# Other places for the low weight blocks of a split float32 matmul, and another order of its three products

## The chip, the cores and the metric

The kernel runs on one core of one Trainium2 chip. The metric is the device time of one execution in microseconds. Before the change it is 2366.06 us, the median of 3 runs that lie between 2365.84 and 2366.32 us.

## The reference

A trunk of two layers works on 256 tokens and 16 learned meta tokens of width 2048. Every layer projects with one combined matrix, runs two groups of attention heads side by side (bidirectional gated linear attention in chunks, and neighbourhood attention on a 64-wide grid), projects back, and follows with a squared-ReLU MLP. Cut to what matters:

```python
def _layer(h, w_in, gla_w_up, gla_b_up, gla_norm_w, na_rel_bias, w_out,
           ln1_w, ln1_b, w_ff1, w_ff2, ln2_w, ln2_b):
    proj = jnp.einsum('bld,dp->blp', h, w_in)
    ...
    gq, gk, gv, gr, glr, nq, nk, nv = jnp.split(proj, points, axis=-1)
    y_gla = _gla_mixer(gq, gk, gv, gr, glr, gla_w_up, gla_b_up, gla_norm_w)
    y_na = _na_mixer(nq, nk, nv, na_rel_bias).astype(h.dtype)
    mix = jnp.einsum('blm,md->bld', jnp.concatenate([y_gla, y_na], axis=-1), w_out)
    h = _layer_norm(DEEPNORM_ALPHA * h + mix, ln1_w, ln1_b)
    ff = jnp.einsum('blf,fd->bld', jnp.square(jax.nn.relu(jnp.einsum('bld,df->blf', h, w_ff1))), w_ff2)
    return _layer_norm(DEEPNORM_ALPHA * h + ff, ln2_w, ln2_b)
```

The four large weights are 2048 x 6176, 2048 x 2048, 2048 x 8192 and 8192 x 2048 per layer, all float32. The meta tokens are dropped from the output, so the second layer needs its result for the 256 tokens alone.

## The kernel before

**Splitting.** Every large product runs on TensorE in the type float32r, with both operands split into a high part (the value cast to float32r) and a low part (the value less its high part). Three products are summed in PSUM: high weights by high activations, high weights by low activations, low weights by high activations.

**Weight tiles.** The weights come from HBM in tiles of 128 partitions x 1024 float32 (`WB`), eight blocks of 128 columns. `order` (line 149) yields them in the order of use and `weights` (line 168) keeps the tile in use and the one after it made. `made` (line 174) starts the DMA into `raw` from SyncE's queue, has ACT cast `raw` into `wh` (line 180) and DVE subtract `wh` from `raw` into `wl` (line 181). Each of `raw`, `wh` and `wl` has three buffers in the pool `wst`, so a buffer is written again when the third tile before it has been used. `head` (line 186) does the same for the very first tile, together with two chunks of the input.

**Where things lie.** In `wh` and in `wl` block j stands at element 128 j, and each tile begins at a multiple of 256 bytes; so every block does. An activation chunk (`x`, `y` or `u`, 128 partitions) is a `Pair` of a high and a low part in one tile. In layer one, and for some products of layer two, the low part begins 288 elements (`PITCH`, 1152 bytes) after the high part. For most of layer two the pair is dense: 256 high columns, then 256 low ones, which one matmul can read as 512.

**Products.** Three functions issue them, all for one weight tile at a time.
- `eight` (line 205) has eight chunks by one output block, and is called by `by_m` (line 253). Where all 272 columns (tokens and meta tokens) are wanted, each chunk has two high products of 272 columns, on line 216: the weights' high block by the chunk's high part, then the same block by its low part. After these 16 come 8 low products on line 219, the low blocks by the high parts. Where 256 columns suffice (`once`, layer two), each chunk has one high product of 512 columns, on line 213, and after these 8 come 8 low products of 256 columns, on line 219, into the right half of the PSUM bank; `whole` or the eviction adds both halves.
- `by_k` (line 232) has two chunks by four (or eight) output blocks, for the first products after a normalisation, on line 246. Its order is its own.

A few calls use 274 or 258 columns, where two more carry a gain and a bias.

**Around them.** `by_m` evicts each finished block with ACT and DVE and calls `pump`, which hands out steps of two queues of generators (`fg`, `bg`): gates, attention, normalisation. Those steps are issued after the last subtraction into `wl` (`issue_after(self.wl)`), so a tile's split stands ahead of them in the queues.

Of the kernel before, what the change touches and what calls it, by code (L numbers as in the profile page):

```python
# [19 lines left out]
L = T + NM  # L20
DEPTH = 2
# [5 lines left out]
WB = 1024  # L27
# [10 lines left out]
MEET = 2  # L38
PAD = 40
PITCH = 288  # L40


class Pair(tuple):
# [10 lines left out]
class Trunk:  # L54
# [95 lines left out]
    def order(self):  # L150

        i, first = self.i, [(), (WB // 2, WB)]
        for l in range(DEPTH):
            groups = [i["win"][l, g] for g in range(12)] + [i["wout"][l, g] for g in range(4)]
            for half in range(2):
                groups += [i["wff1"][l, 8 * half + g] for g in range(8)] + [i["wff2"][l, half, g] for g in range(4)]
            if l == 0:
                for t in range(groups[0].shape[0]):
                    for w in groups[:2]:
                        yield w[t], first.pop(0) if first else (WB,)  # L160
                groups = groups[2:]
            for w in groups:
                for t in range(w.shape[0]):
                    yield w[t], (WB,)

    def weights(self):

        while len(self.ready) < 2:
            self.ready.append(self.made(*next(self.stream, (None, ()))))
        return self.ready.popleft()  # L170

    def made(self, ap, ends):
        if ap is None:
            return None
        nc = self.nc
        raw, wh, wl = (self.wp.tile([P, WB], d, name=nm, tag=nm)
                       for nm, d in (("raw", F32), ("wh", F32R), ("wl", F32R)))
        for c in map(slice, (0,) + ends, ends):
            nc.sync.dma_start(raw[:, c], ap[:, c])
            nc.scalar.copy(wh[:, c], raw[:, c])  # L180
            self.wl = nc.vector.tensor_tensor(wl[:, c], raw[:, c], wh[:, c].bitcast(F32), ALU.subtract).ins  # L181
        if not ends:
            self.head(ap, raw, wh, wl)
        return wh, wl

    def head(self, ap, raw, wh, wl):

        nc, q = self.nc, WB // 4
        both = self.xr.tile([P, 2, q + L], F32, name="head", tag="head", bufs=1)
        self.x[:2] = [self.pair(self.xp, "x", c) for c in range(2)]  # L190
        for c in range(2):
            nc.sync.dma_start(both[:, c], self.i["head"][:, c])
        nc.sync.dma_start(raw[:, 2 * q:], ap[:, 2 * q:])
        for c in range(2):
            at = slice(c * q, c * q + q)
            h, lo = (t[:, :L] for t in self.x[c])
            todo = [(both[:, c, q:], h, lo), (both[:, c, :q], wh[:, at], wl[:, at])]
            for args in todo[::-1] if c else todo:
                self.split(*args)
        for at in (slice(2 * q, 3 * q), slice(3 * q, WB)):  # L200
            nc.scalar.copy(wh[:, at], raw[:, at])
            self.wl = nc.vector.tensor_tensor(wl[:, at], raw[:, at], wh[:, at].bitcast(F32), ALU.subtract).ins

    def eight(self, ps, wh, wl, x, n, first, last, once):

        mm = self.nc.tensor.matmul
        c = lambda w, j: w[:, j * P:j * P + P]  # L210
        for j, v in enumerate(x):
            if once:
                mm(ps, lhsT=c(wh, j), rhs=v.once, start=first and not j, stop=False)  # L213
                continue
            for i in range(2):
                mm(ps[:, :n], lhsT=c(wh, j), rhs=v[i][:, :n], start=first and not i + j, stop=False)  # L216
        o = ps[:, T:] if once else ps[:, :n]
        for j, (h, _) in enumerate(x):
            mm(o, lhsT=c(wl, j), rhs=h[:, :T if once else n], start=False, stop=last and j == 7)  # L219

    def whole(self, parts):

# [7 lines left out]
    def by_k(self, acts, n, before, wide=False):  # L230

        ps = [self.pm.tile([P, 512], F32, name="mm", tag="mm") for _ in range(4)]
        if wide:
            ps += [self.bank() for _ in range(4)]
        nk = len(acts)
        for k in range(0, nk, 2):
            before(k)
            for g in range(0, len(ps), 4):
                wh, wl = self.weights()
                parts = ((wh, 0), (wh, 1), (wl, 0))  # L240
                order = [(j, p, m) for j in range(2) for p in range(3) for m in range(4)]
                by_output = k == nk - 2 or k == 0 and not wide
                order.sort(key=lambda o: (o[0], o[2] // 2) if wide and not k + g else (by_output and o[2], o[1] // 2))
                for j, p, m in order:
                    c = j * 512 + m * P
                    self.nc.tensor.matmul(ps[g + m][:, :n], lhsT=parts[p][0][:, c:c + P], rhs=acts[k + j][parts[p][1]][:, :n],  # L246
                                          start=k + j + p == 0, stop=k == nk - 2 and j + p == 3)
        return [p[:, :n] for p in ps]

# [930 lines left out]
```

## Time and profile before

| | |
|---|---|
| median of 3 runs | 2366.06 us |
| the profiled execution, whole | 2366.29 us |
| its span | 2364.5 us |
| instructions | 44607 |
| matmuls, and as many weight loads | 18180 |
| TensorE busy | 2356.2 us |
| VectorE (DVE) busy | 1520.8 us |
| ScalarE (ACT) busy | 1219.3 us |
| HBM read, mean over the span | 414.03 MB, 176 GB/s |

A row of a group gives the line of the kernel, the engine, the operation, output and inputs by the program's names, the shapes, the count; then busy time in us and the mean duration of one in ns; then the engine's idle time just before them and what ended it. PE is TensorE's matmuls, PEld its weight loads, which run beside matmuls. Matmuls are pipelined: one starts long before the one ahead of it has ended, so their durations do not add up, and a group's busy time is the union. In the order of time a row gives the start in us, the time from the first start to the last end, and the instructions merged into it; the distance between the starts of two rows that follow each other on an engine tells what the first one cost. Rows of one source line give the least, the median and the greatest duration.

### The profile page before, as it was taken

What the parts mean: (1) busy time and instruction counts of PE and PEld (TensorE: products, weight loads), DVE (VectorE), ACT (ScalarE), POOL (GpSimd) and SP (SyncE); (2) the same over time, 40 slices, a digit from 0 to 9 for tenths busy, and PEclk for the clock granted to TensorE, in tenths of its full rate; (3) what the DMA queues carried; (4) which work ended last, traced back from release to release, by engine and by line L of the source; (5) the groups of instructions that cost most, each with busy time, mean ns of one, the idle gap of its engine ahead of it and who ended that gap; (6) DMA issues with size and microseconds to landing.
All of it is one profiled execution on the core that took longest, in us unless ns stands there. A gap on an engine that the chain in (4) does not pass through costs nothing.

```text
span 2364.5 us, 44607 instructions
## 1 busy us (share of the span) xinstructions
PE 2356.2 (100%) x18180; PEld 2241.9 (95%) x18180; DVE 1520.8 (64%) x2432; ACT 1219.3 (52%) x2100; POOL 136.2 (6%) x200
## 2 busy tenths in 40 slices
PE   9999999999999999999999999999999999999998
PEld 9999999999999999999999899999988888888888
DVE  5588777775544455546576787778766455666654
ACT  5666664564433344444456666655644333444443
POOL 0021100100000000000030111101100000000000
PEclk9999999999999999999999999999999999999999
DMA  7454445555555555555555555455566666556664
GB/s 261 153 160 153 156 135 176 173 176 178 177 178 176 176 177 179 177 177 174 177 184 171 164 160 165 155 160 188 187 192 190 189 187 188 188 190 212 195 188 144
DMA packets 118301, 419.02 MB, mean 177 GB/s; under 512 B 13512, under 2 KB 14024, under 8 KB 118096
## 3 DMA queue, kind: packets, MB, share of 16 engines
q1 hardware_dynamic: 117808, 415.65, 55.8%
q8 instruction: 142, 2.33, 0.4%
q14 instruction: 63, 0.52, 0.1%
q10 hardware_dynamic: 288, 0.52, 0.1%
HBM read 414.03 MB, written 2.10 MB: 176 GB/s over the span
## 4 chain that ended last, share of the span: by engine, by line
PE 98%; DVE 1%; issue 0%; ACT 0%; POOL 0%; DVEq 0%; ACTq 0%; POOLq 0%
PE mm L216 35%; PE mm L219 29%; PE mm L213 22%; PE mm L246 6%; PE bg L246 1%; PE bg L757 1%; PE mm L696 1%; PE bg L557 0%; PE bg L403 0%; DVE wl L181 0%; PE mm L722 0%; PE mm L446 0%; PE bg L883 0%; PE bg L608 0%; PE bg L638 0%
## 5 line engine op out<-in xcount | busy, mean ns | idle before, releaser
L181 DVE TENSOR_TENSOR wl<-raw,wh 128x1024 fp32r<-128x1024 f32 (+1 forms) x768 | 941.8, 1227 | 621.5 <-ACT wh L180 618.4
L180 ACT CAST wh<-raw 128x1024 fp32r<-128x1024 f32 (+1 forms) x768 | 803.5, 1047 | 919.4 <-PE mm L216 367.7
L216 PE MATMUL mm<-x,wh 128*128 128x272 f32 (+2 forms) x4224 | 569.8, 287 | 0.0
L216 PEld LDWEIGHTS mm<-x,wh 128*128 128x128 f32 x4224 | 541.1, 188 | 0.8 <-PE mm L696 0.2
L219 PE MATMUL mm<-x,wl 128*128 128x272 f32 (+3 forms) x3264 | 466.9, 285 | 0.0
L219 PEld LDWEIGHTS mm<-x,wl 128*128 128x128 f32 x3264 | 437.5, 189 | 11.6
L213 PE MATMUL mm<-x,wh 128*128 128x512 f32 x1152 | 290.1, 394 | 0.0
L213 PEld LDWEIGHTS mm<-x,wh 128*128 128x128 f32 x1152 | 207.2, 189 | 37.9 <-PE mm L696 0.4
L219 PE MATMUL mm<-y,wl 128*128 128x272 f32 (+1 forms) x1408 | 200.5, 285 | 0.0
L219 PEld LDWEIGHTS mm<-y,wl 128*128 128x128 f32 x1408 | 189.5, 189 | 6.5
L216 PE MATMUL mm<-y,wh 128*128 128x272 f32 (+1 forms) x1440 | 193.3, 286 | 0.0
L216 PEld LDWEIGHTS mm<-y,wh 128*128 128x128 f32 x1440 | 184.3, 188 | 0.0
L213 PE MATMUL mm<-y,wh 128*128 128x512 f32 x688 | 172.6, 392 | 0.0
L219 PE MATMUL mm<-u,wl 128*128 128x272 f32 (+1 forms) x1024 | 145.8, 285 | 0.0
L213 PEld LDWEIGHTS mm<-y,wh 128*128 128x128 f32 x688 | 123.6, 189 | 21.9
L219 PEld LDWEIGHTS mm<-u,wl 128*128 128x128 f32 x1024 | 137.8, 189 | 4.8
L216 PE MATMUL mm<-u,wh 128*128 128x272 f32 (+1 forms) x1056 | 141.2, 286 | 0.0
L216 PEld LDWEIGHTS mm<-u,wh 128*128 128x128 f32 x1056 | 134.9, 188 | 0.0
L213 PE MATMUL mm<-u,wh 128*128 128x512 f32 x496 | 124.2, 392 | 0.0
L213 PEld LDWEIGHTS mm<-u,wh 128*128 128x128 f32 x496 | 89.2, 189 | 15.9
L246 PE MATMUL mm<-x,wh 128*128 128x272 f32 (+1 forms) x512 | 73.3, 288 | 0.0
L246 PEld LDWEIGHTS mm<-x,wh 128*128 128x128 f32 x512 | 67.9, 191 | 0.0
(273 smaller groups left out, 1856.5 us busy)
## 6 DMA issues: line engine op xcount, KB each, us to landing
raw<-in_wff SPq DMA_DIRECT2D x512, 512.0 KB, 3.6
raw<-in_win SPq DMA_DIRECT2D x190, 512.0 KB, 3.8
raw<-in_wout SPq DMA_DIRECT2D x64, 512.0 KB, 3.6
nb<-in_nab SPq DMA_DIRECT2D x16, 352.0 KB, 4.7
xraw<-in_xT SPq DMA_DIRECT2D x7, 272.0 KB, 5.2
out<-out SPq DMA_DIRECT2D x5, 256.0 KB, 3.2
brow<-in_norm SPq DMA_DIRECT2D x4, 256.0 KB, 4.8
gw<-in_wup SPq DMA_DIRECT2D x4, 196.0 KB
```

The lines of the kernel that those rows point to most:

```text
L180: nc.scalar.copy(wh[:, c], raw[:, c])
L181: self.wl = nc.vector.tensor_tensor(wl[:, c], raw[:, c], wh[:, c].bitcast(F32), ALU.subtract).ins
L213: mm(ps, lhsT=c(wh, j), rhs=v.once, start=first and not j, stop=False)
L216: mm(ps[:, :n], lhsT=c(wh, j), rhs=v[i][:, :n], start=first and not i + j, stop=False)
L219: mm(o, lhsT=c(wl, j), rhs=h[:, :T if once else n], start=False, stop=last and j == 7)
L246: self.nc.tensor.matmul(ps[g + m][:, :n], lhsT=parts[p][0][:, c:c + P], rhs=acts[k + j][parts[p][1]][:, :n], start=k + j + p == 0, stop=k ...
L696: nc.tensor.matmul(ps[hh][:, t * NKEY:t * NKEY + NKEY], lhsT=q[hs, NM + t * P:NM + t * P + P], rhs=k[hs, t, :], start=True, stop=True)
L757: nc.tensor.matmul(po[t][hs, :P], lhsT=v2[ts, hs] if rest else v1[:, t, hs], rhs=p2[ts, hh, :] if rest else p1[:, 2 * hh + t, :], start=re ...
```

## The change

`wl` becomes 1280 elements wide (`WIDE`), and the low blocks no longer stand side by side. A tile that only serves products of 512 and 256 columns (`once`) has its low blocks 16 elements from the start, with steps of 160 in a pair and 320 from pair to pair: at 64 and 192 bytes by turns, counted within 256 bytes. All other tiles have them at 0, 176, 320, 496 and so on: at 0 and 192 bytes by turns. The high blocks stay side by side.

So that `made` knows which layout to use, `order` yields with every tile whether it is `once`. The cast and the subtraction are written for pairs of blocks (`halves`, `pairs`), and the products take a block's address from `block`.

The order in `eight` comes from a string. For `once` it is as before, eight high products (`h`) and eight low ones (`w`). For the others it was 16 high products and then 8 low ones; now two chunks have their four high products (`h` with the chunk's high part, `l` with its low part) and then their two low ones (`w`), four times over. The order in `by_k` is as before; its low blocks have new places too.

The three wider buffers take 3 KB more of each partition. `dynamic_dma_scratch_size` goes from 8192 to 2048, which moves all tiles by a multiple of 256 bytes.

```diff
+WIDE = 1280
+LOWS = {True: (16, P + 32, 2 * P + 64), False: (0, P + 48, 2 * P + 64)}
+TURNS = {True: "hhhhhhhhwwwwwwww", False: "hlhlwwhlhlwwhlhlwwhlhlww"}
...
-    def made(self, ap, ends):
+    def made(self, ap, ends, once):
...
-        raw, wh, wl = (self.wp.tile([P, WB], d, name=nm, tag=nm)
-                       for nm, d in (("raw", F32), ("wh", F32R), ("wl", F32R)))
+        raw = self.wp.tile([P, WB], F32, name="raw", tag="raw")
+        wh, wl = self.wp.tile([P, WB], F32R, name="wh", tag="wh"), self.wp.tile([P, WIDE], F32R, name="wl", tag="wl")
+        wh, wl = self.blocks(wh, 0, P, 2 * P), self.blocks(wl, *LOWS[once])
         for c in map(slice, (0,) + ends, ends):
             nc.sync.dma_start(raw[:, c], ap[:, c])
-            nc.scalar.copy(wh[:, c], raw[:, c])
-            self.wl = nc.vector.tensor_tensor(wl[:, c], raw[:, c], wh[:, c].bitcast(F32), ALU.subtract).ins
+            self.halves(raw[:, c], wh, wl, slice(c.start // P, c.stop // P))
...
+    def blocks(self, flat, first, step, pair):
+
+        ap = lambda at, n: bass.AP(flat.tensor, flat.offset + first + at, [flat.ap[0]] + n + [[1, P]])
+        return ap, step, pair
+
+    def block(self, w, j):
+        ap, step, pair = w
+        return ap(j // 2 * pair + j % 2 * step, [])
+
+    def pairs(self, w, at):
+
+        ap, step, pair = w
+        return ap(at.start // 2 * pair, [[pair, (at.stop - at.start) // 2], [step, 2]])
+
+    def halves(self, src, wh, wl, at):
+        h, lo = (self.pairs(w, at) for w in (wh, wl))
+        r = src.rearrange("p (g b c) -> p g b c", b=2, c=P)
+        self.nc.scalar.copy(h, r)
+        self.wl = self.nc.vector.tensor_tensor(lo, r, h.bitcast(F32), ALU.subtract).ins
...
     def eight(self, ps, wh, wl, x, n, first, last, once):
...
-        c = lambda w, j: w[:, j * P:j * P + P]
-        for j, v in enumerate(x):
+        seen = dict.fromkeys("hlw", 0)
+        for i, kind in enumerate(TURNS[once]):
+            j = seen[kind]
+            seen[kind] += 1
+            w, v, o = wl if kind == "w" else wh, x[j], ps[:, :n]
+            rhs = v[kind == "l"][:, :n]
             if once:
-                mm(ps, lhsT=c(wh, j), rhs=v.once, start=first and not j, stop=False)
-                continue
-            for i in range(2):
-                mm(ps[:, :n], lhsT=c(wh, j), rhs=v[i][:, :n], start=first and not i + j, stop=False)
-        o = ps[:, T:] if once else ps[:, :n]
-        for j, (h, _) in enumerate(x):
-            mm(o, lhsT=c(wl, j), rhs=h[:, :T if once else n], start=False, stop=last and j == 7)
+                rhs, o = (v.once, ps) if kind == "h" else (v[0][:, :T], ps[:, T:])
+            mm(o, lhsT=self.block(w, j), rhs=rhs, start=first and not i, stop=last and i == len(TURNS[once]) - 1)
...
-    nc = bacc.Bacc("TRN2", target_bir_lowering=False, num_devices=1, dynamic_dma_scratch_size=8192)
+    nc = bacc.Bacc("TRN2", target_bir_lowering=False, num_devices=1, dynamic_dma_scratch_size=2048)
```

More of the change, by code (lines that the diff above doesn't have):

```diff
@@ L153, in order @@
         for l in range(DEPTH):
[L154 removed]
+            last = l + 1 == DEPTH
+            na = [last and c % 3 == 0 for c in range(24)]
+            groups = [(i["win"][l, g], [last and g in (2, 4, 5)] * 4 if g < 6 else na[4 * g - 24:4 * g - 20]) for g in range(12)]
+            groups += [(i["wout"][l, g], [last and g > 0] * 4) for g in range(4)]
             for half in range(2):
[L156 removed]
+                groups += [(i["wff1"][l, 8 * half + g], [last and (half > 0 or g > 2)] * 4) for g in range(8)]
+                groups += [(i["wff2"][l, half, g], [last] * 4) for g in range(4)]
             if l == 0:
[L158 to L160 removed]
+                for t in range(groups[0][0].shape[0]):
+                    for w, _ in groups[:2]:
+                        yield w[t], first.pop(0) if first else (WB,), False
                 groups = groups[2:]
[L162 to L164 removed]
+            for w, once in groups:
+                n = w.shape[0]
+                for t in range(n):
+                    yield w[t], (WB,), once[4 * t // n]
     def weights(self):
         while len(self.ready) < 2:
[L169 removed]
+            self.ready.append(self.made(*next(self.stream, (None, (), False))))
         return self.ready.popleft()
[L172 removed]
+    def made(self, ap, ends, once):
         if ap is None:
@@ L244, in by_k @@
                 for j, p, m in order:
[L245 to L246 removed]
+                    self.nc.tensor.matmul(ps[g + m][:, :n], lhsT=self.block(parts[p][0], 4 * j + m), rhs=acts[k + j][parts[p][1]][:, :n],
                                           start=k + j + p == 0, stop=k == nk - 2 and j + p == 3)
```

14 lines of the change are left out of this document (7 added, 7 removed).

## The prediction

> **What bounds the kernel now.** I read the page first, then the groups of instructions on TensorE with shapes kept apart, then the lines of the products one by one, then the order of time inside single weight tiles.
>
> ```profile
> span 2364.5 us, 44607 instructions
> PE 2356.2 (100%) x18180; PEld 2241.9 (95%) x18180; DVE 1520.8 (64%) x2432; ACT 1219.3 (52%) x2100; POOL 136.2 (6%) x200
> ...
> PEclk9999999999999999999999999999999999999999
> ...
> PE 98%; DVE 1%; issue 0%; ACT 0%; POOL 0%; DVEq 0%; ACTq 0%; POOLq 0%
> ```
>
> TensorE has no idle time worth the name, its clock is granted throughout, and the chain that ended last is TensorE for 98%. So an edit on another engine pays nothing unless it makes TensorE wait, and an edit on TensorE pays exactly what it takes off the distance from one matmul's start to the next. The products that the change touches are these:
>
> ```profile
> L216 PE MATMUL mm<-x,wh 128*128 128x272 f32 x3584 | 483.1, 287 | 0.0
> L213 PE MATMUL mm<-x,wh 128*128 128x512 f32 x1152 | 290.1, 394 | 0.0
> L219 PE MATMUL mm<-x,wl 128*128 128x272 f32 x1792 | 260.3, 287 | 0.0
> L216 PE MATMUL mm<-y,wh 128*128 128x272 f32 x1408 | 189.1, 286 | 0.0
> L213 PE MATMUL mm<-y,wh 128*128 128x512 f32 x688 | 172.6, 392 | 0.0
> L219 PE MATMUL mm<-x,wl 128*128 128x256 f32 x1152 | 160.4, 282 | 0.0
> L216 PE MATMUL mm<-u,wh 128*128 128x272 f32 x1024 | 137.1, 286 | 0.0
> L213 PE MATMUL mm<-u,wh 128*128 128x512 f32 x496 | 124.2, 392 | 0.0
> L219 PE MATMUL mm<-y,wl 128*128 128x272 f32 x704 | 102.3, 287 | 0.0
> L219 PE MATMUL mm<-y,wl 128*128 128x256 f32 x704 | 98.2, 282 | 0.0
> L219 PE MATMUL mm<-u,wl 128*128 128x272 f32 x512 | 74.4, 287 | 0.0
> L219 PE MATMUL mm<-u,wl 128*128 128x256 f32 x512 | 71.4, 282 | 0.0
> ```
>
> That is 6016 high products of 272 columns, 3008 low ones of 272, 2336 high ones of 512 and 2368 low ones of 256. Their mean durations overlap, since matmuls are pipelined, so the distance between starts has to come from the order of time. First a tile of layer one, then one of layer two:
>
> ```profile
> 686.63 1.16 PE L219 MATMUL mm<-y,wl 128*128 128x272 f32 x8
> 686.83 1.05 ACT L180 CAST wh<-raw 128x1024 fp32r<-128x1024 f32 x1 [1.93 <-PE mm L216]
> ...
> 687.63 2.14 PE L216 MATMUL mm<-y,wh 128*128 128x272 f32 x16
> 687.91 1.23 DVE L181 TENSOR_TENSOR wl<-raw,wh 128x1024 fp32r<-128x1024 f32 x1 [1.49 <-ACT wh L180]
> ...
> 689.61 1.16 PE L219 MATMUL mm<-y,wl 128*128 128x272 f32 x8
> ...
> 690.61 0.29 PE L216 MATMUL mm<-u,wh 128*128 128x272 f32 x1
> ...
> 1817.12 2.00 PE L213 MATMUL mm<-y,wh 128*128 128x512 f32 x8
> ...
> 1818.96 1.12 PE L219 MATMUL mm<-y,wl 128*128 128x256 f32 x8
> ...
> 1819.91 0.40 PE L213 MATMUL mm<-u,wh 128*128 128x512 f32 x1
> ```
>
> From start to start: 16 high products of 272 in 1.98 us are 124 ns each, 8 low ones in 1.00 us are 125 ns, 8 of 512 in 1.84 us are 230 ns, and 8 low ones of 256 in 0.95 us are 119 ns. Each is its mean duration less about 162 ns, so a nanosecond off a duration is a nanosecond off the path. From 256 to 512 columns the price rises by 111 ns, or 0.43 ns a column; 272 columns at that rate are 118 ns and 256 are 111, so 7 to 10 ns of every product are not its columns. And equal products differ:
>
> ```profile
> L219 PE MATMUL mm<-y,wl x1408: 277/283/296, 374.3 to 2345.5; 128*128 128x272 f32 x88, 128*128 128x256 f32 x88
> ...
> L219 PE MATMUL mm<-u,wl x1024: 277/284/296, 644.9 to 2351.2; 128*128 128x272 f32 x86, 128*128 128x256 f32 x85
> ...
> L216 PE MATMUL mm<-y,wh x1440: 283/288/291, 372.3 to 2344.5; 128*128 128x272 f32 x176, 128*128 128x256 f32 x4
> ...
> L216 PE MATMUL mm<-u,wh x1056: 283/288/290, 642.9 to 2350.3; 128*128 128x272 f32 x171, 128*128 128x256 f32 x5
> ...
> L213 PE MATMUL mm<-y,wh x688: 388/392/398, 1565.0 to 2333.1; 128*128 128x512 f32 x172
> ...
> L213 PE MATMUL mm<-u,wh x496: 389/391/398, 1819.9 to 2338.6; 128*128 128x512 f32 x166
> ```
>
> Least, median and greatest duration are shown. One form, one clock, no wait, and yet 388 to 398 ns, or 283 to 291. Something small and regular costs TensorE up to 10 ns a product. What differs between such products is which addresses are read, and when: the moving operand of one product and the weights of the next are read at the same time. That is the only thing that the change can buy.
>
> **The change, part by part.** No instruction is added or taken away: the same products, casts, subtractions and DMAs, so the count terms are zero.
>
> The split into high and low writes the low half in runs of 128 with gaps of 32 or 48 elements. The nearest rows:
>
> ```profile
> L181 DVE TENSOR_TENSOR wl<-raw,wh 128x1024 fp32r<-128x1024 f32 x766 | 940.4, 1228 | 621.4 <-ACT wh L180 618.3 <-PE bg L883 1.7
> ...
> L911 DVE TENSOR_TENSOR s<-s,sqv 128x272 f32<-128x272 f32 x30 | 13.0, 435 | 0.0
> ...
> L681 DVE TENSOR_TENSOR ns<-ns,nst 128x512 f32<-128x512 f32 x16 | 11.1, 693 | 0.5
> ```
>
> From 272 to 1024 contiguous elements DVE pays 1.05 ns an element, so 512 would cost 688 ns; line 681, which writes four runs of 128 out of rows of 176, takes 693. Gaps cost nothing there. Even at 10% more the split stays hidden, for DVE idles 621 us ahead of it. I take nothing.
>
> Low products after every two chunks, where a product has 272 columns (24 products in place of 16 high, then 8 low). The low half is now wanted by the 5th product, not the 17th: 12 x 124 ns = 1.49 us sooner. The subtraction at 687.91 fills the buffer of the tile that ended at 687.63, so it is for the third tile after that one, whose products start at about 693.6. It ends at 689.14 and is wanted at 694.1, 5.0 us later. The high buffer is read until the 22nd product, not the 16th, so the cast that waits for it (idle 1.93 us) starts 0.74 us later; behind it on ACT stand evictions, and the subtraction follows, which leaves 4.2 us. The tightest place I found is the switch from 512 to 272 columns in layer two:
>
> ```profile
> 1286.72 1.23 DVE L181 TENSOR_TENSOR wl<-raw,wh 128x1024 fp32r<-128x1024 f32 x1 [0.15 <-ACT wh L180]
> ...
> 1287.46 2.17 PE L216 MATMUL mm<-x,wh 128*128 128x272 f32 x16
> ```
>
> The low half is ready at 1287.95 and would be wanted at 1287.46 + 0.50 = 1287.96. No cover is left there: if the subtraction slips, TensorE waits, by at most about 1.5 us, once. I take 0 to 2 us, and 0 as the value.
>
> Other places for the low blocks (and the regrouping's effect on who reads when). The trace has no low block off a multiple of 256 bytes, so this is bounded from both sides by the spread of equal products. If every product fell to the least of its form: high 272 from 287 or 286 to 283, 3584 x 4 + 2432 x 3 ns = 21.6 us; low 272 to the same 283, 3008 x 4 = 12.0 us; low 256 from 282 to 277, 2368 x 5 = 11.8 us; 512 from 394 or 392 to 389, 1152 x 5 + 1184 x 3 = 9.3 us. Together 54.7 us, and no more can be got. If all rose to the greatest (291, 296, 296 for 272 low, 398 for 512): 6016 x 4 + 3008 x 9 + 1152 x 4 + 1184 x 6 = 63 us lost, without the 256s.
>
> The Trainium skill's page "SBUF — State Buffer", section "Who interferes with whom", gives TensorE two independent read ports, one for moving data and one for weights, and says that PE never waits on anyone. By that rule the placement is worth 0 and the time stays. Its section "Door 1" counts a line as 16 bytes, and all these offsets are multiples of that, so that rule too gives 0. The spread quoted above is what this trace holds against it.
>
> I take about half of the bound, by the median of u's 512s: 391, with 389 the least, so half of these already pay 2 ns or less, and cheap meetings of the two reads are ordinary. Low 256: 3 of 5 ns, 7.1 us. 512, whose own weights do not move and which gain only by when they start: half, 4.6 us. Low 272: 3 of 4 ns, 9.0 us. High 272, three quarters of whose following loads stay put: 1.5 ns, 9.0 us. Sum 29.7 us.
>
> The profiled execution took 2366.29 us, its span 2364.5 and 1.8 around it; it stands 0.2 above the median of 2366.06. 2366.3 - 29.7 = 2336.6, so 2336 to 2337 on the median's scale. I say 2336.5.
>
> **Rivals.**
>
> Placement is worth nothing. The 7 to 10 ns could be a fixed price of swapping weights, the same wherever they lie. For it: every product has its own load, even two in a row with the same weights, and the loads are busy 95%. Against it: a fixed price has no spread of 10 ns. The time would be 2366, with 0 to 2 us for the tight tile. The port rule of the Trainium skill above says the same.
>
> A worse meeting of the two reads. The same mechanism with the other sign: the low 272s, which reach 296 now against a mean of 287, land nearer the top because the offset differs by 64 bytes from one low block to the next and the order puts each pair of low loads among high ones. It decides once the mean of the low 272s passes 287. Half way to 296 is 4.5 x 3008 = 13.5 us: 2380. For it: nothing in the rows says which offset is the good one. Against: the present places are not good either, with means 3 to 5 ns over the least in all four forms, so there is as much room to fall as to rise, and two offsets by turns break up a pattern in which every load meets the same place.
>
> The low half comes late. If the subtraction slips behind other DVE work where tiles follow each other closely, as at 1287, TensorE waits 1.5 us a tile; ten such tiles are 15 us, with no gain 2381. Against: the ordinary lead is over 4 us, and the quoted groups of products show 0.0 us of idle time before them.
>
> **How the numbers follow.** Gain from placement and order 0.69, within it the forecast at 2336.5 and its own range 2312 (the bound: 2366.3 - 54.7) to 2358; placement worth nothing 0.07; a worse meeting 0.20; low half late 0.04. About 0.2%, 4.7 us, is what a measurement of this kernel tells from no change. Faster 0.69, same 0.07, slower 0.24. For 8 in 10 the range runs from the bound, 2312, to 2378, which takes in no change and most of the worse meetings.
>
> **What would show it.** Right: TensorE stays at 100% with no idle before the low products; the mean durations of the low forms fall from 287 and 282 to about 284 and 279, the high 272s to 285, the 512s to 390; eight products plus eight of layer two take less than 2.79 us from start to start, the 24 of layer one less than 2.98. Wrong in size: the means fall in one layer only. Wrong in sign: the mean of the low 272s over 287, or idle time before low products with DVE's subtraction named as releaser. DVE's mean of 1228 for the split should stand; if it grows by more than a tenth, the gaps cost something after all.

## The result, and the profile after

The changed kernel takes 2360.56 us (median of 11 runs, 2360.02 to 2361.41), the kernel before 2366.32 us (11 runs, 2365.62 to 2367.19). The ratio is 0.9976, with a 95% interval from 0.9967 to 0.9985: faster by 5.8 us. I had said faster by about 30.

From the page of the profiled execution after the change: its span, the engines and the chain of work that ended last.

```profile
span 2358.4 us, 44599 instructions
PE 2348.3 (100%) x18180; PEld 2234.0 (95%) x18180; DVE 1523.6 (65%) x2432; ACT 1213.4 (51%) x2100; POOL 131.4 (6%) x200
...
PE 97%; DVE 2%; issue 1%; ACT 1%; POOL 0%; DVEq 0%; ACTq 0%; POOLq 0%
```

The split after the change, from the groups with shapes kept apart:

```profile
L212 DVE TENSOR_TENSOR wl<-raw,wh 128x1024 fp32r<-128x1024 f32 x766 | 940.5, 1229 | 648.2 <-ACT wh L211 643.7 <-PE mm L472 2.1 <-PE mm L722 0.3
```

TensorE is still busy throughout, so the gain is again in how far apart its products start. The split that now leaves gaps, on line 212, takes 1229 ns on average for a whole tile, as against 1228 before: the gaps cost VectorE nothing.

The groups of products after the change, shapes kept apart (`eight` is now on line 246, `by_k` on line 272; the last three numbers are busy time in us, mean of one in ns, idle time before):

```profile
L246 PE MATMUL mm<-x,wh 128*128 128x272 f32 x3584 | 595.4, 288 | 0.0
L246 PE MATMUL mm<-x,wl 128*128 128x272 f32 x1792 | 367.5, 286 | 0.0
L246 PE MATMUL mm<-x,wh 128*128 128x512 f32 x1152 | 289.8, 394 | 0.0
L246 PE MATMUL mm<-y,wh 128*128 128x272 f32 x1408 | 233.8, 288 | 0.0
...
L246 PE MATMUL mm<-x,wl 128*128 128x256 f32 x1152 | 156.6, 278 | 0.0
L246 PE MATMUL mm<-y,wl 128*128 128x272 f32 x704 | 144.5, 287 | 0.0
...
L246 PE MATMUL mm<-y,wl 128*128 128x256 f32 x704 | 96.0, 277 | 0.0
```

Busy times of the 272s can't be compared with those of before: a group's busy time is a union, and in the new order its stretches are shorter and overlap those of the other group. The means can. Low 256 went from 282 to 277 and 278, nearly all that I had called possible (9.7 of 11.8 us by the table further down). Low 272 went from 287 to 286 or not at all, 512 did not move, and high 272 rose from 287 and 286 to 288.

The order of time shows it from start to start. A stretch of layer one, then one of layer two, after the change:

```profile
685.76 0.67 PE L246 MATMUL mm<-y,wh 128*128 128x272 f32 x4
686.27 0.41 PE L246 MATMUL mm<-y,wl 128*128 128x272 f32 x2
...
688.76 0.66 PE L246 MATMUL mm<-y,wh 128*128 128x272 f32 x4
689.26 0.41 PE L246 MATMUL mm<-y,wl 128*128 128x272 f32 x2
...
691.76 0.66 PE L246 MATMUL mm<-u,wh 128*128 128x272 f32 x4
...
1813.11 2.00 PE L246 MATMUL mm<-x,wh 128*128 128x512 f32 x8
1814.94 1.08 PE L246 MATMUL mm<-x,wl 128*128 128x256 f32 x8
1815.86 2.00 PE L246 MATMUL mm<-y,wh 128*128 128x512 f32 x8
```

A layer-one tile of 24 products now takes 3.00 us (685.76 to 688.76, and again to 691.76), where it took 2.98 before. In layer two, 8 products of 512 take 1.83 us, the 1.84 of before within the rounding, and 8 low ones 0.92 us where they took 0.95. So the change wins in layer two and loses a part of that in layer one.

TensorE also waits where it didn't before. Its waits before and then after the change, with the total, the number and the longest in us:

```profile
PE bg L372 <- DVE zero L369: 1.2, 1, 1.2
PE bg L883 <- ACT sp L268: 0.7, 1, 0.7
PE bg L883 <- DVE sp L269: 0.3, 1, 0.3
```

```profile
PE mm L472 <- ACT ft L459: 1.2, 2, 0.6
PE bg L398 <- DVE zero L395: 1.2, 1, 1.2
PE bg L909 <- ACT sp L294: 0.8, 1, 0.8
PE mm L272 <- DVE wl L212: 0.6, 1, 0.6
PE bg L909 <- DVE sp L295: 0.3, 1, 0.3
```

The second, third and fifth of these were there before, on lines 372 and 883. The first and the fourth are new: transposes in `v_rows` that wait for an eviction on ScalarE, and a low product in `by_k` that waits for its split.

### The profile page after: what moved, and what is told of

It is laid out like the page before. It is cut to its first block, busy times and chain, and to the rows that moved or that the text cites. A ratio compares the mean times of both kernels' runs of the same rounds, so it can differ in the third digit from the quotient of the medians.

```text
span 2358.4 us, 44599 instructions
## 1 busy us (share of the span) xinstructions
PE 2348.3 (100%) x18180; PEld 2234.0 (95%) x18180; DVE 1523.6 (65%) x2432; ACT 1213.4 (51%) x2100; POOL 131.4 (6%) x200
## 4 chain that ended last, share of the span: by engine, by line
PE 97%; DVE 2%; issue 1%; ACT 1%; POOL 0%; DVEq 0%; ACTq 0%; POOLq 0%
PE mm L246 85%; PE mm L272 6%; PE bg L272 1%; PE bg L783 1%; PE mm L722 1%; PE bg L583 0%; DVE wl L212 0%; PE bg L429 0%; PE mm L748 0%; DVE acc L1011 0%; ACT wh L211 0%; PE mm L472 0%; PE bg L909 0%; PE bg L634 0%; PE bg L664 0%
## 5 line engine op out<-in xcount | busy, mean ns | idle before, releaser
L246 PE MATMUL mm<-x,wh 128*128 128x272 f32 (+3 forms) x5376 | 990.5, 311 | 0.0
L246 PEld LDWEIGHTS mm<-x,wh 128*128 128x128 f32 x5376 | 798.4, 188 | 38.6 <-PE mm L722 0.6
L246 PE MATMUL mm<-x,wl 128*128 128x272 f32 (+3 forms) x3264 | 590.1, 284 | 0.0
L246 PEld LDWEIGHTS mm<-x,wl 128*128 128x128 f32 x3264 | 485.4, 188 | 11.4
L246 PE MATMUL mm<-y,wh 128*128 128x272 f32 (+2 forms) x2128 | 411.4, 322 | 0.0
L246 PE MATMUL mm<-u,wh 128*128 128x272 f32 (+2 forms) x1552 | 299.1, 321 | 0.0
L246 PE MATMUL mm<-y,wl 128*128 128x272 f32 (+1 forms) x1408 | 240.5, 282 | 0.0
L272 PEld LDWEIGHTS mm<-x,wh 128*128 128x128 f32 x512 | 67.9, 191 | 0.0
L999 POOL TENSOR_SCALAR acc<-acc,vec 128x272 f32<-128x272 f32 (+1 forms) x24 | 41.9, 1751 | 273.9 <-DVE acc L1011 154.2
L560 ACT COPY U<-S 128x272 f32<-128x272 f32 (+1 forms) x104 | 41.0, 429 | 19.3 <-DVE S L569 18.3
L569 DVE TENSOR_TENSOR S<-S,dec 128x272 f32<-128x272 f32 (+1 forms) x112 | 46.1, 441 | 3.7 <-ACT U L560 3.1
```

The source lines that it names most:

```text
L246: mm(o, lhsT=self.block(w, j), rhs=rhs, start=first and not i, stop=last and i == len(TURNS[once]) - 1)
L272: self.nc.tensor.matmul(ps[g + m][:, :n], lhsT=self.block(parts[p][0], 4 * j + m), rhs=acts[k + j][parts[p][1]][:, :n], start=k + j + p == ...
L560: nc.scalar.copy(U[:, lv % 4, j, :w].rearrange("p (n t h) -> p n t h", t=2, h=hb), bass.AP(S.tensor, S.offset + 2 * j * L, [S.ap[0], [2 * ...
L569: tt(o, o, totals(lv, odd, w), ALU.mult)
L999: nc.gpsimd.tensor_scalar(a, a, gain, bias, ALU.mult, ALU.add)
```

## The experiments

All kernels below are the changed kernel with one or two of its lines other than they are; each diff is against it. "Old order" means this line in place of the changed one:

```diff
-TURNS = {True: "hhhhhhhhwwwwwwww", False: "hlhlwwhlhlwwhlhlwwhlhlww"}
+TURNS = {True: "hhhhhhhhwwwwwwww", False: "hlhlhlhlhlhlhlhlwwwwwwww"}
```

`True` stands for the tiles of 512 and 256 columns (layer two), `False` for all others (layer one and the rest). In `LOWS` the three numbers are the first element, the step to the second block of a pair, and the step from pair to pair. 64, 128 and 192 bytes are 16, 32 and 48 elements. The kernel before took 2366.4 to 2366.5 us beside all of them.

### The parts of the change one by one

Layer two's places alone: old order, and

```diff
-LOWS = {True: (16, P + 32, 2 * P + 64), False: (0, P + 48, 2 * P + 64)}
+LOWS = {True: (16, P + 32, 2 * P + 64), False: (0, P, 2 * P)}
```

> Only the low blocks of the once tiles (layer two) move, to 64 and 192 bytes by turns; all other tiles and the order of the products are as before. Theory: the gain comes from these places alone and the rest of the change gives part of it back, so the low products of 256 columns start 115 ns apart in place of 119.5 and the time is about 2356.5 us, 10 us under the kernel before and 4 under the changed one. Rival: the gain in layer two needs the regrouped order or the new places of the other tiles around it (where each product starts), and the time stays near 2360 to 2366.

Measured: 2355.96 us, ratio 0.9956 (0.9943 to 0.9970), 10.5 us faster than before and 4.6 faster than the whole change. The low products of 256 columns and a stretch of layer two in its trace:

```profile
L246 PE MATMUL mm<-x,wl 128*128 128x256 f32 x1152 | 156.5, 278 | 0.0
...
L246 PE MATMUL mm<-y,wl 128*128 128x256 f32 x704 | 95.0, 277 | 0.0
...
L246 PE MATMUL mm<-u,wl 128*128 128x256 f32 x512 | 69.1, 277 | 0.0
```

```profile
1813.23 1.08 PE L246 MATMUL mm<-y,wl 128*128 128x256 f32 x8
1814.14 2.00 PE L246 MATMUL mm<-y,wh 128*128 128x512 f32 x8
1815.98 1.08 PE L246 MATMUL mm<-y,wl 128*128 128x256 f32 x8
```

With one order throughout, the busy times can be compared with the rows of before: 160.4, 98.2 and 71.4 us have become 156.5, 95.0 and 69.1, which is 9.4 us less in all. That is nearly the whole gain. 8 of 512 still take 1.84 us. The kernels further down share the wider buffers and the smaller scratch with this one, and where they keep layer two's low blocks at multiples of 256 bytes (the order alone, the places 0 and 192 alone), its low products take 119.5 ns from start to start as before; here they take 115.4. So the bytes at which these blocks lie make the gain, and "placement is worth nothing" is out.

The order alone: all low blocks at multiples of 256 bytes, new order.

```diff
+LOWS = {True: (0, P, 2 * P), False: (0, P, 2 * P)}
```

> Only the order of the 272-column products is new (low ones after every two chunks); every low block is where it was before, in a buffer 1280 wide. Theory: the order by itself costs, since the high products of layer one rose by 1.3 ns and the low ones fell by 1.4 in the whole change, 5376 against 2688 of them: about +3 us, 2369. Rival: the order is what pays for the low products and the places 0 and 192 are what costs: 2362 to 2364.

Measured: 2371.33 us, ratio 1.0021 (1.0012 to 1.0030): the order costs 4.9 us. When it is paid can be read from the high products of `u`. The first and last starts of their rows, first in the kernel before, then with the order alone:

```profile
L216 PE MATMUL mm<-u,wh x1056: 283/288/290, 642.9 to 2350.3; 128*128 128x272 f32 x171, 128*128 128x256 f32 x5
```

```profile
L246 PE MATMUL mm<-u,wh x1552: 283/288/398, 644.9 to 2355.6; 128*128 128x272 f32 x128, 128*128 128x512 f32 x62, 128*128 128x256 f32 x4
```

2.0 us are lost by 643 us and 5.3 by the end. (The second row counts more, since it takes in the 512s; the first and the last product are the same in both, for the kernel before issues its last 512 of `u` at 2338.6.) TensorE's waits in this run:

```profile
PE mm L472 <- ACT ft L459: 1.2, 2, 0.6
...
PE mm L272 <- DVE wl L212: 0.2, 1, 0.2
```

1.4 us of the 4.9 are waits that the kernel before does not have. The 1.2 us on line 472 come with the order: no kernel here in the old order has them. The 0.2 on line 272 may not, for the old order with layer two's places alone, and with the places 0 and 192 alone, waits 0.3 and 0.4 us for a cast there. Of the rest, 2.2 us are slower products, as the table below shows.

The places 0 and 192 alone: old order, layer two as before.

```diff
+LOWS = {True: (0, P, 2 * P), False: (0, P + 48, 2 * P + 64)}
```

> Only the low blocks of the other tiles (mostly layer one) move, to 0 and 192 bytes by turns, with 16 high and then 8 low products as before. Theory (order costs, places pay or do nothing): 2362 to 2366. Rival (places cost): 2368 to 2372, with the mean of the low 272s over 287.

Measured: 2367.35 us, ratio 1.0006 (0.9997 to 1.0015). These places give nothing. By the medians they cost 0.9 us, which the interval doesn't tell from no change.

Layer two's places and the new order together, without 0 and 192:

```diff
+LOWS = {True: (16, P + 32, 2 * P + 64), False: (0, P, 2 * P)}
```

> Low blocks of layer two at 64 and 192 bytes by turns and the new order, but the low blocks of all other tiles back at multiples of 256 bytes: the change without its places 0 and 192. If the parts add up (layer-two places -10.5 us, order +4.9), 2360.9 us, and the places 0 and 192 are worth 0 under the new order as under the old one (+0.9). If the new order only pays with the places 0 and 192, as a rival could say, this is 2363 or more; if these places do harm under the new order, 2358 or less.

Measured: 2361.14 us, ratio 0.9978 (0.9969 to 0.9987), where the sum of the two parts says 2360.9. The parts add up, and 0 and 192 are worth 0.6 us under the new order, which is inside the intervals. So the change is three things: -10.5 us for layer two's places, +4.9 for the order, about nothing for the places elsewhere.

### Where the time of the products went

A group's mean in ns is too coarse for effects of 1 ns in 5000 products, so I took every matmul record's start and the start of the next one, and averaged over each form. The first two columns of numbers are high and low products of 272 columns in layer one, the next two those of 512 and 256 in layer two, in ns; the last column is the change of all other matmuls against before, waits among them, in us.

```
                                 h272   l272   h512   l256   others
count                            5376   2688   2336   2368
before                          124.2  125.5  230.8  119.5
the change                      125.5  124.1  230.6  115.4   +0.8
layer two's places alone        124.1  125.5  230.6  115.4   -0.2
order alone                     125.4  123.9  230.8  119.5   +2.5
places 0 and 192 alone          124.3  125.5  230.8  119.5   -0.1
layer two: all at 64            124.2  125.5  230.4  118.3   +0.5
layer two: 0 and 128            124.2  125.5  231.6  118.4   -0.1
layer two: 192 and 64 (clean)   124.2  125.5  230.7  118.6   +1.8
layer one: 64 and 192           124.6  125.8  230.6  115.5   -0.1
layer one: all at 128           125.2  126.2  230.6  115.5   -0.4
layer one: 0 and 128            125.6  125.6  230.6  115.5   +1.5
high blocks 64 and 192          124.2  125.5  231.0  117.1    0.0
high blocks 0 and 128           124.2  125.5  233.0  117.0   -0.2
high and low by turns           124.1  125.5  235.2  118.3    0.0
four chunks, then four lows     125.3  124.0  230.6  115.5   +1.1
layer two's places, new order   125.4  123.9  230.6  115.4   +3.0
layer two: 192 and 64 (flawed)  124.7  125.6  231.0  117.5   +0.3
```

The order alone makes 5376 high products 1.2 ns slower (+6.5 us) and 2688 low ones 1.6 ns faster (-4.2 us): 2.2 us net, beside 2.5 in the others, 1.4 of them the waits. What the other 1.1 us are stays open.

The means hide a pattern. Averaged by place in the tile, over the 250 tiles of layer two whose pairs are dense and into which no other matmul falls, the distances to the next start are, in ns, for the eight 512s and then the eight low 256s:

```
                            512, one to eight                                low 256, one to eight
before                      233.3 235.8 228.3 232.5 230.8 226.7 226.7 226.7  113.3 119.2 120.0 120.0 120.0 120.0 120.0 120.0
layer two's places alone    232.5 235.8 228.3 232.5 230.8 226.7 226.7 225.8  117.5 115.8 114.2 113.3 113.3 113.3 113.3 113.3
```

So a low product at a multiple of 256 bytes isn't dear by itself: the first one, behind the 512s, takes 113.3 ns, and 120.0 is what the others settle at behind each other. With 64 and 192 bytes they settle at 113.3.

Nor do these places pay everywhere. In the first 40 tiles of layer two with 512 columns `x` still has its low part 1152 bytes after the high one. There the low 256s take 122.3 ns before and 122.4 with layer two's places alone; in the 252 tiles with dense pairs they take 119.1 and 114.3. More of the attention's matmuls come between in those 40, but in the 28 without any the low 256s take 118.3 ns in both kernels. This points to the layout of the activations as a second condition; no run changed it by itself. Such a tile with layer two's places, where eight low ones still take 0.95 us:

```profile
1286.21 1.11 PE L246 MATMUL mm<-x,wl 128*128 128x256 f32 x8
1287.16 1.03 PE L246 MATMUL mm<-x,wh 128*128 128x272 f32 x7
```

### Other places in layer two

All with the old order and layer one as before; the low blocks all at 64 bytes:

```diff
+LOWS = {True: (16, P, 2 * P), False: (0, P, 2 * P)}
```

> As the first kernel, but with every low block of a once tile at 64 bytes, none at 192. If it is the offset against the moving operand that counts, the low 256s fall as with 64 and 192 by turns, to about 115 ns, and the time is about 2356. If it is the turn from one place to the next that counts, they stay near 119 ns and the time near 2365.

Measured: 2363.13 us, ratio 0.9985 (0.9977 to 0.9994): a third of the gain.

At 0 and 128 by turns:

```diff
+LOWS = {True: (0, P + 32, 2 * P + 64), False: (0, P, 2 * P)}
```

> Layer two's low blocks at 0 and 128 bytes by turns, the same step between neighbours as 64 and 192, but 64 bytes lower; all else as in the kernel with layer two's places alone (2356.0). If the turn of 128 bytes from one load to the next is what pays, the low 256s stay at about 115 ns and the time at 2356. If the distance to the moving operand, which begins at 0, counts as well, they rise to between 117 and 119.5 ns: 2360 to 2366.

Measured: 2365.66 us, ratio 0.9995 (0.9987 to 1.0004): the distance of 128 bytes between neighbours alone is not what pays. The 256s gained 2.7 us and the 512s, whose own blocks did not move, lost 1.9.

At 192 and 64 by turns, the same two places in the other order, in buffers of 1312 elements:

```diff
-WIDE = 1280
-LOWS = {True: (16, P + 32, 2 * P + 64), False: (0, P + 48, 2 * P + 64)}
+WIDE = 1312
+LOWS = {True: (48, P + 32, 2 * P + 64), False: (0, P, 2 * P)}
```

> Layer two alone, with its low blocks at 192 and 64 bytes by turns in place of 64 and 192, old order, other tiles as before. If what counts is that neighbours differ by 128 bytes and none stands on a multiple of 128, the same gain of 10.5 us: 2356.0 us. If the first low block of a tile must stand in a certain place to the high blocks ahead of it, part of the gain goes: 2359 to 2363 us.

Measured: 2366.02 us, ratio 0.9998 (0.9989 to 1.0007), no gain. But layer one's high 272s, which should not have moved, took 124.7 ns in place of 124.2, 3.1 us in all. The experiment was flawed: 1312 elements are 5248 bytes, 20.5 times 256, so one low buffer of three, and what stands behind it, moved by 128 bytes.

The flaw tells something all the same. In every third tile the low blocks lay at 64 and 192 bytes after all, and the chunks `u`, which lie behind the weight buffers, began 128 bytes off, while `x` and `y`, ahead of them, did not move. Among the dense tiles without other matmuls, every third one with `y` takes 114.3 ns for a low 256, as with layer two's places alone. With `u` the same places take 118.6, where layer two's places alone give 114.3. So the place of the moving operand counts with that of the weights. The distance between the two is not all either: in the other tiles with `u` the distances are 64 and 192 bytes again, and they take 118.3 and 116.7 ns, like the other tiles with `y`.

The run was repeated with 1344 elements (21 times 256), beside a control, layer two's places alone in the same wider buffers:

```diff
+WIDE = 1344
+LOWS = {True: (48, P + 32, 2 * P + 64), False: (0, P, 2 * P)}
```

> The run with 192 and 64 bytes by turns had low buffers of 1312 elements, 5248 bytes, which is 20.5 times 256: one buffer of three, and what stands behind it, moved by 128 bytes, and layer one got slower by 3 us though its order and its steps were as before. Here the buffers have 1344 elements, 21 times 256 bytes, so that only layer two's places differ from before. If what counts is that neighbours differ by 128 bytes and none stands on a multiple of 128, 2356.0 us and the low products of 256 columns at 277 to 278 ns. If their phase counts, 2359 to 2363 us and 279 to 281 ns.

```diff
+WIDE = 1344
+LOWS = {True: (16, P + 32, 2 * P + 64), False: (0, P, 2 * P)}
```

> The best version so far (layer two's low blocks at 64 and 192 bytes by turns, all else as before) with buffers of 1344 elements in place of 1280: both are multiples of 256 bytes. If only the place within 256 bytes counts, 2356.0 us as before. If which multiple of 256 bytes a buffer begins at counts too, another time, by a microsecond or more.

Measured: 2364.12 us, ratio 0.9990 (0.9982 to 0.9999), for 192 and 64; 2356.03, ratio 0.9955 (0.9941 to 0.9969), for the control, the 2355.96 of above again. The low products with 192 and 64:

```profile
L246 PE MATMUL mm<-x,wl 128*128 128x256 f32 x1152 | 159.1, 280 | 0.0
...
L246 PE MATMUL mm<-y,wl 128*128 128x256 f32 x704 | 97.5, 280 | 0.0
```

So the buffers' length made no difference as long as it was a multiple of 256 bytes, and the place within 256 bytes did, including which of two places comes first: 64 before 192 is worth 10.5 us, 192 before 64 2.3 us. Neither of my two explanations for layer two (neighbours at a distance of 128 bytes; none on a multiple of 128) tells these apart. Why the first place matters stays open.

### Other places in layer one

All three with layer two's good places and the old order, so that the measure is 2355.96. First 64 and 192 there too, then all low blocks at 128, then 0 and 128:

```diff
+LOWS = {True: (16, P + 32, 2 * P + 64), False: (16, P + 32, 2 * P + 64)}
```

> 64 and 192 bytes by turns in every tile, the old order in all. If these places are good wherever low loads follow each other, the eight low 272s of a tile fall by the same 4 ns from 125 to 121, 3008 of them, and the time is about 2344. [...]

```diff
+LOWS = {True: (16, P + 32, 2 * P + 64), False: (32, P, 2 * P)}
```

> Layer two's places, and every low block of the other tiles at 128 bytes, old order. 0 costs 125.5 ns for a low 272, 0 and 192 by turns 125.5, 64 and 192 125.8. If 272 columns have no good place for a low load, the time stays within 2354 to 2360; if the eight low ones have a chain without a meeting, they fall towards 121 ns and the time to 2344.

```diff
+LOWS = {True: (16, P + 32, 2 * P + 64), False: (0, P + 32, 2 * P + 64)}
```

> As the one before, with 0 and 128 bytes by turns for the other tiles. Same two readings: 2354 to 2360, or towards 2344.

Measured: 2359.57 (ratio to before 0.9971, 0.9959 to 0.9982), 2364.08 (0.9990, 0.9982 to 0.9999) and 2365.33 us (0.9997, 0.9988 to 1.0005), so 3.6, 8.1 and 9.4 us worse than with layer one left alone. Two tiles of layer one with all low blocks at 128:

```profile
687.48 2.17 PE L246 MATMUL mm<-y,wh 128*128 128x272 f32 x16
689.49 1.17 PE L246 MATMUL mm<-y,wl 128*128 128x272 f32 x8
690.50 2.15 PE L246 MATMUL mm<-y,wh 128*128 128x272 f32 x16
692.49 1.17 PE L246 MATMUL mm<-y,wl 128*128 128x272 f32 x8
```

Both last runs lie outside what I had expected. 16 high products take 2.01 and 1.99 us here, where they took 1.98, though their own blocks lie where they lay. The place of the low blocks changes the price of high products too. Of the five placements tried in layer one, the one of before is the best or level with the best.

### High blocks, and other orders

On top of layer two's places alone, the high blocks of the same tiles moved as well, to 0 and 128 bytes by turns, or to 64 and 192:

```diff
-wh, wl = self.blocks(wh, 0, P, 2 * P), self.blocks(wl, *LOWS[once])
+wh, wl = self.blocks(wh, *((0, P + 32, 2 * P + 64) if once else (0, P, 2 * P))), self.blocks(wl, *LOWS[once])
```

> As the kernel with layer two's places alone, with the high blocks of once tiles too at places by turns (0 and 128 bytes, in a buffer 1280 wide). The 512s stand at 230.6 ns against 227 for the cheapest of them. If the meeting of two reads sets them, they change by at least 1 ns either way: 2348 to 2354, or 2359 and more. If they only depend on being the first after the low ones, they stay and the time is 2356.

```diff
+wh, wl = self.blocks(wh, *((16, P + 32, 2 * P + 64) if once else (0, P, 2 * P))), self.blocks(wl, *LOWS[once])
```

> Layer two's low places, and the high blocks of once tiles at 64 and 192 bytes by turns as well (they were worse at 0 and 128: 2365.2). If 64 and 192 are good against a moving operand that begins at 0, for high loads as for low ones, the 512s fall from 230.6 towards 227 ns: 2336 of them, up to 8.4 us, 2348 to 2352. If the 512s keep 8 and 11 more ticks only because they come first after the low ones, they stay and the time is 2356. If high loads have another good place, 2358 and more.

Measured: 2365.18 us (ratio 0.9995, 0.9986 to 1.0004) and 2360.76 (0.9977, 0.9967 to 0.9986): 9.2 and 4.8 us of the gain lost. The places that are good for low blocks are not good for high ones, and part of the price falls on products that did not move: with the high blocks at 64 and 192 the low 256s lose 4.0 us (117.1 ns in place of 115.4) and the 512s 1.0; at 0 and 128 they lose 3.6 and 5.7. (The 8 and 11 ticks of the last expectation are presumably the 6.6 and 9.1 ns that the first two 512s of a tile cost more than the last ones, 233.3 and 235.8 in place of 226.7 in the kernel before.)

On top of layer two's places alone, high and low products by turns in layer two:

```diff
+TURNS = {True: "hw" * 8, False: "hlhlhlhlhlhlhlhlwwwwwwww"}
```

> Layer two's places as in the changed kernel, but each high product of 512 followed by its low product of 256, so that every low load lies beside a 512 and every high load beside a 256. By the meeting of reads a chain of equal products settles into a good or a bad phase, and a mixed one changes phase with every product: the gain of the low 256s is lost at least in part, 2360 to 2370. If only the place of a low block counts, whatever its neighbours: 2356.

Measured: 2373.44 us, ratio 1.0029 (1.0018 to 1.0039). That is more than I had expected: the low 256s lose most of their gain (118.3 ns), and the 512s rise to means of 398 and 397 ns:

```profile
L246 PE MATMUL mm<-x,wh 128*128 128x512 f32 x1152 | 407.8, 398 | 0.0
L246 PE MATMUL mm<-y,wh 128*128 128x512 f32 x688 | 244.0, 397 | 0.0
```

And four chunks together in layer one in place of two:

```diff
+TURNS = {True: "hhhhhhhhwwwwwwww", False: "hlhlhlhlwwwwhlhlhlhlwwww"}
```

> Layer two's places only, and the 272-column products in groups of four chunks (eight high, four low, twice a tile). The order of two chunks alone cost 4.9 us. If what costs is each turn from high to low products (four turns a tile for two chunks, two here, one before) the cost here is a third, 1.6 us on 2356.0: 2357 to 2358.5. If it is any departure from the settled pattern of high pairs, the cost stays near 5: 2360 to 2362. If it is the high buffer that is given back later (22nd product for two chunks, 20th here, 16th before), about two thirds: 2359.

Measured: 2359.68 us, ratio 0.9972 (0.9962 to 0.9983), 3.7 us over the old order in the same places. Its waits for line 459 come to 0.7 us in place of 1.2. By the table the 272s cost 2.3 us net, as much as with two chunks, so the number of turns from high to low is not what they pay for; the others fall from 2.5 us to 1.1, which fits the high buffer that is given back earlier. All high products and then all low ones, as before, is the best order of those tried, and the kernel with layer two's places alone is the fastest, level with its control.

## Why the prediction had the sign and missed the size

**What bounds the kernel** held. TensorE stayed at 100%, and every nanosecond off a start-to-start distance came off the end: the columns of the table, summed with "others", give -6.1 us for the change, and the times differ by 5.8.

**The split's gaps** at no cost held (1229 ns, as against 1228).

**The spread of equal products has to do with addresses** held: layer two's places alone gave 10.5 us. That the price comes from the meeting of two reads, the moving operand's and the next weights', is not shown: the flawed run and the first tiles of layer two speak for it, but no run moved the moving operand alone. (The "7 to 10 ns" beyond the columns are 6 to 8 by the figures beside them; the sum doesn't use them.) The rule of the Trainium skill that I had set against it ("SBUF — State Buffer", "Who interferes with whom": independent read ports, TensorE waits on nobody) would have had 0 there. The time, 2355.96 for 2366.4, decides against 0 for these operands.

**"I take about half of the bound"** is the step that failed. I had a bound of 54.7 us from the least duration of each form, and halved it in all four forms without a row that said that any of them would move. Term by term, from the table: low 256 forecast at -7.1 us, measured -9.7 (2368 times 4.1 ns), mis-sized a little; 512 forecast at -4.6, measured -0.5; low 272 forecast at -9.0, measured -3.7 in layer one; high 272 forecast at -9.0, measured +7.0. The first term was too small, the second and third too large, and the fourth had the wrong sign. The reason I gave for taking half, that half of `u`'s 512s already pay little, says that cheap meetings exist, not that the new places bring more of them.

What the runs show in place of chance meetings is a fixed sequence. Besides layer two's, shown by place above, the high 272s of layer one before the change take 121 and 126 ns by turns from the fourth product of a tile on, and of the eight low ones the second takes 133.4 (its durations are the 296 in the rows), over 304 tiles without other matmuls. So the least of a form belongs to a place in the tile, and the rows don't say whether the other places can reach it. The low 256s did: five of eight came down to 113.3. The others did not: on average over a kernel, 8 products of 512 never took less than the 1.84 us of before, and layer one's 272s in no place or order came to fewer ns in all than they had, but for 0.1 us of 1000. The new order breaks the turns of 121 and 126 up, and the high 272s get dearer.

**The order** I had costed at 0 for itself, with a tight place that might cost up to 2 us. It costs 4.9, nearly half in slower products, and the waits fell elsewhere than I looked. I had written that the cast starts later and that evictions stand behind it on ScalarE, and had then followed only the split. The place where that bites is the end of layer two's 272s, seen after the change:

```profile
1316.70 1.04 ACT L211 CAST wh<-raw 128x1024 fp32r<-128x1024 f32 x1 [1.95 <-PE mm L246]
1316.71 0.49 PE L472 MATMUL mm<-ident,ft 128*128 128x128 f32 x3
1317.13 0.33 PE L583 MATMUL bg<-qk 128*32 128x32 f32 x16
1317.65 0.38 ACT L459 COPY ft<-mm 128x272 f32<-128x272 f32 x1
...
1318.09 0.55 PE L472 MATMUL mm<-ident,ft 128*128 128x128 f32 x3 [0.63 <-ACT ft L459]
```

and with layer two's places alone, in the old order:

```profile
1310.68 1.17 PE L246 MATMUL mm<-x,wl 128*128 128x272 f32 x8
1310.92 1.05 ACT L211 CAST wh<-raw 128x1024 fp32r<-128x1024 f32 x1 [1.93 <-PE mm L246]
1311.69 0.49 PE L472 MATMUL mm<-ident,ft 128*128 128x128 f32 x3
1311.88 0.39 ACT L459 COPY ft<-mm 128x272 f32<-128x272 f32 x1
```

In the old order the cast is released when the 16 high products are done, runs beside the 8 low ones, and the eviction of the finished block starts at 1311.88, 0.19 us after the transposes begin. In the new order the last high product is the 22nd of 24, the cast starts at 1316.70 as the tile ends, holds ScalarE for 1.04 us, and the eviction starts 0.94 us after the transposes began. The transposes of the second block then stand for 0.63 us. The tight place that I had named, the switch from 512 to 272 columns, shows up in no wait of line 246.

**The rivals.** "Placement is worth nothing" fell. "A worse meeting" was right in kind for layer one, where every other place tried in the old order costs from about nothing to 9.4 us, but not by its sign of 287 for the low 272s: they did not get worse under the change, the high ones did. "The low half comes late" described a path that exists (0.6 us on line 272, and the eviction's 1.2), where I had written 15.

Not settled: what in the reads sets the sequence of prices, why high 272s lose and low ones gain when they stand closer together, and why 64 before 192 is better than 192 before 64.

## What to carry to other kernels

When equal products differ by a few ns with no wait in sight, the bytes within 256 at which the weights begin are worth trying, but one form at a time: here 64 and 192 by turns took 4 ns off each low product of 256 columns on average, and cost time with the 272s and with the high blocks. Look at equal products by their place in the tile before calling their spread chance. A bound from least durations shows what some place in the tile reaches, and not what will come to the others; without a row that ties an edit to a form, its term is 0 with the bound as the range's end. When an order moves the last reader of a buffer, follow everything that stands behind the released instruction on its engine, at the ends of stretches as well as in their middle.

## What the hardware showed that I had not expected

The place within 256 bytes of a block of weights bears on how closely matmuls follow each other: 8 low products of 256 columns took 0.95 us with all blocks at multiples of 256 and 0.91 with 64 and 192 by turns. The price also falls on neighbours whose own operands did not move: layer one's high products went from 124.2 to 125.2 ns when the low blocks went to 128 bytes. A product's price also hangs on the products ahead of it: at multiples of 256 bytes the first low 256 behind the 512s took 113.3 ns and the last six 120.0. And a buffer's length counts: low buffers of 5248 bytes, by themselves and by what they push 128 bytes on, cost layer one 3 us, while 5120 and 5376 bytes, both multiples of 256, gave 2355.96 and 2356.03 us.
